# A hybrid decoder layer on one core: the attention projection cut into 32 pieces inside the recurrence, with other loads for the merge and another form of the last layer norm

## Chip, core and metric

The kernel runs on one core of a Trainium2 chip. The metric is the device time of one execution in microseconds (us), the median of several runs. All data is fp32; dense products are done as three products of a split in two parts (high and low).

## The reference, cut to what matters

One layer is computed for a prompt of 512 tokens and for 8 sequences of 4 tokens (32 sample tokens), 544 columns in all, model width 1024:

```
x = LN1(alpha*x + 1/2*gate1*SwiGLU_1(mod1(x)))
u = mod2(x);  proj = u @ w_in + b_in
y_a = rwkv7_time_mix(...)            # 8 heads x 64, recurrent state
y_b = nsa attention(...)             # 8 query heads x 64
m = (sigmoid(gA)*(y_a @ w_out_a) + sigmoid(gB)*(y_b @ w_out_b)) @ w_o
x = LN2(alpha*x + gate2*m)
x = LN3(alpha*x + 1/2*gate3*SwiGLU_2(mod3(x)))
layer_norm(x) = (x - mean) * rsqrt(var + eps) * g + b      # over the 1024 features
```

`y_a @ w_out_a` and `y_b @ w_out_b` have an inner width of 512 (four tiles of 128); SwiGLU's inner width is 2816.

## The kernel before

Activations are held feature by token: a tile has 128 features as partitions and 544 tokens as columns. A dense product of one output tile (`dense`, `dense_half`) loads a weight tile, splits it into a high part (cast on ScalarE) and a low part (subtraction on VectorE, `split`), and does three products per inner tile, on 272 columns at a time.

The program is written as generators, and the Tile framework orders each engine's instructions by a simulated list schedule: of the instructions that are ready in its model, the one first in program order goes first. On the chip each engine, and each DMA queue (SP's, ScalarE's, POOL's), then takes its instructions strictly in that order.

**Recurrence.** Four generators (`rw_head`), each for two heads of the time mixing, run interleaved, a new one starting nine steps after the last. In one of them `rw_prompt` has four solving steps (`k4`: selection products, then small VectorE operations, L1645 to L1665), steps of small 32x32 products (L1687, L1695, L1713), products of state (L1733 to L1764), a scan of seven steps (`c`: L1780, then one VectorE operation), and a tail of group norm (`rw_tail`) that ends with the split of the result into `yah`. Every step takes PSUM tiles of one bank from `smp` (`sm()`, four banks, 41 such tiles a generator) or of two banks from `mmp` (`mm()`, two buffers).

**Attention projection.** `wob_steps` (L1945 to L1980) computes, for each of 8 output tiles n, `y_b @ w_out_b` in two halves of 272 columns, each of twelve products (four inner tiles by three), evicts each with one VectorE operation (`stt`, which also applies the gate in the tile `gst`) and stores the result to DRAM (`mbd[n]`, on SP's queue). It is a generator of 16 pieces; the main loop takes a piece whenever a step of a head says `yield True`, with `high_priority(offset=300)`. Three steps of `rw_prompt` say so (after L1687, L1695 and L1713), so that 12 pieces go beside the heads and 4 (48 products) follow the loop.

**Merge.** After the recurrence `merge_load(n)` loads a tile of `w_out_a`, the gate `gdr[0, n]` and `mbd[n]`. The products (`merge_part`, L2040) of tiles 0 and 1 begin with the inner tiles 0 to 2 and end with tile 3. Each n then has two VectorE operations with the gate and `mbd`, and a split into `u`; `xT` (the residual) is loaded beside it, and the products with `w_o` follow (`last_product`, L288). The pools lie one behind the other in SBUF: the merge's `u` lies where the recurrence's `f` and sample tiles lay, its `gate` and `mb` tiles where the mask constants and the `e` tiles (the tail's) lay, `xT` where the attention's result `ybh` lay.

**Last norm.** In the last product of the second SwiGLU the columns are done in two halves of 272. `LayerNormOut` transposes each finished feature tile to tokens (L710), collects `bn_stats` (L712), and `finish` evicts each tile of tokens in two halves: ScalarE applies mean and rstd, VectorE multiplies by g (L730), POOL or VectorE adds b (L731), SP stores (L732). For the second half three tiles of tokens (two of 128, one of 32) end together after the last product.

Of the kernel before, what the change touches and what calls it, by code (L numbers as in the profile page):

```python
# [17 lines left out]
D = 1024  # L18
# [111 lines left out]
def build(tc, I, O, upto=99, dbg=None):  # L130
# [28 lines left out]
    def sm(shape=(128, 512), tag="sm"):  # L159
        return smp.tile([128, 512], F32, tag=tag, name=nm("sm"))  # L160
# [133 lines left out]
    def v272(t):  # L294
        return t.rearrange("p (a b) -> p a b", a=2)
# [313 lines left out]
    HT = TOK // 2  # L609

    def ln_prep(wk, k, h, run):

# [78 lines left out]
    class LayerNormOut:  # L691


        def __init__(self, wk, i):
            self.wk, self.t = wk, {}
            self.gb = [wk.tile([128, D], F32, name=f"lno{j}") for j in range(2)]
            for t, name in zip(self.gb, ("ln_g", "ln_b")):
                src = I[name][0, i]
                SY.dma_start(t, bass.AP(src.tensor, src.offset, [[0, 128], [1, D]]))

        def col(self, tag, n):
            return self.wk.tile([128, n], F32, tag=tag, name=nm(tag), bufs=3)

        def feature(self, qt, k):
            m = 128 if qt < 4 else NS
            if k == 0:
                self.t[qt] = ([sm(), sm()] if qt < 4 else (lambda p: [p[:, 0, :], p[:, 1, :]])(mm()),
                              self.col("lst", 12), m)
            ps, st, m = self.t[qt]
            T.transpose(ps[k // 4][:m, (k % 4) * 128:(k % 4 + 1) * 128], xT[:, k, qt * 128:qt * 128 + m], ident)  # L710
            if k % 4 == 3:
                V.bn_stats(st[:m, 6 * (k // 4):6 * (k // 4) + 6], ps[k // 4][:m])  # L712
            if k == KT - 1:
                self.finish(qt)

        def finish(self, qt):
            ps, st, m = self.t.pop(qt)
# [888 lines left out]
    def rw_prompt(ht, d):  # L1606
# [44 lines left out]
        for k4 in range(4):  # L1651
            ps = sm()
            nk = min(4, 15 - 4 * k4)
            for k in range(nk):
                T.matmul(ps[:, k * 128:(k + 1) * 128], sel[:, 4 * k4 + k, :], dd.rearrange("p q t -> p (q t)"),  # L1655
                         start=True, stop=True)
            for k_ in range(nk):
                k = 4 * k4 + k_
                n = 15 - k
                ab = ps[:, k_ * 128:(k_ + 1) * 128].rearrange("p (q t) -> p q t", t=16)  # L1660
                mul(tmp[:, :, 0:n], ab[:, :, k + 1:], bc(x16[:, :, k:k + 1], [128, 8, n]))
                sub(x16[:, :, k + 1:], x16[:, :, k + 1:], tmp[:, :, 0:n])
# [285 lines left out]
    def wob_steps():  # L1948

        for n in range(KT):  # L1950
# [41 lines left out]
    stu.close()  # L1992
    stw.close()
    yap = pool("yap")
    yah = [yap.tile([128, 4, TOK], F32R, name=f"yah{i}") for i in range(2)]
    str_ = ExitStack()
    wp, wn = pool("wps", stack=str_), 512
    rq = pool("rq", stack=str_)
# [12 lines left out]
                    next(wst, None)  # L2011
    for _ in wst:
        pass
    str_.close()
# [11 lines left out]
    u = new_u()  # L2026

    def merge_load(n):
        raw = load_raw(wview(woa, 0, 512, n * 128, (n + 1) * 128))
        t = [op.tile([128, TOK], F32, tag=tag, name=f"{tag}{n}", bufs=6) for tag in ("gate", "mb")]  # L2030
        SY.dma_start(t[0], gdr[0, n])
        SY.dma_start(t[1], mbd[n])
        return raw, t

    def merge_part(ps, w, k0, k1):
        hv, lv = w
# [4 lines left out]
                             start=(k == 0 and j == 0), stop=(k == 3 and j == 2))  # L2041


    ahead = [merge_load(n) for n in range(3)]
    parts = []
    for n in range(2):
        parts.append((mm(), split(ahead[n][0])))
        merge_part(*parts[n], 0, 3)
    for n in range(KT):
        if n + 3 < KT:  # L2050
            ahead.append(merge_load(n + 3))
        if n < 2:
            ps = parts[n][0]
            merge_part(*parts[n], 3, 4)
        else:
            ps = mm()
            merge_part(ps, split(ahead[n][0]), 0, 4)
        ga, mb = ahead[n][1]
# [49 lines left out]
    stx.close()  # L2108
    es.close()


# [47 lines left out]
```

## Time and profile before

| | us |
|---|---|
| median of 3 runs | 1773.29 |
| lowest, highest | 1766.15, 1776.47 |
| the profiled execution: its run | 1771.6 |
| the profiled execution: its span | 1769.4 |
| TensorE matmul busy in the span | 1666.9 (94%) |
| VectorE, ScalarE, POOL busy | 879.5, 603.1, 242.3 |
| mean granted TensorE clock | 0.974 |

The span runs from the first to the last instruction. Busy time of matmuls is modelled, since they are pipelined; an engine that is busy over the whole span is not one at its peak. PE is TensorE, PEld its weight loads, DVE VectorE, ACT ScalarE. A granted clock of 1.00 is 2.4 GHz, 0.50 is 1.2 GHz.

### The profile page before, as it was taken

Reading aid. Unit: us, or ns where it says so; the run is one execution under the profiler, and the core shown is the slowest. Engines: PE = TensorE matmul, PEld = TensorE weight load, DVE = VectorE, ACT = ScalarE, POOL = GpSimd, SP = SyncE. Lnnn points to the kernel's source line nnn. Section 1 sums busy time; section 2 is a strip of 40 time slices with the busy share of each in tenths; the row PEclk is TensorE's granted clock in tenths of the full one; section 3 lists DMA queues with packets and bytes.
Section 4 is the critical chain, followed back from the end, with each engine's and each line's share of the span. In section 5 each row is a group of like instructions: output and inputs, shape, how many; then the busy total and the mean of one; then the engine's idle time right before and its main releaser. Section 6 shows DMA issues by size and latency. Waiting matters only on the chain.

```text
span 1769.4 us, 34773 instructions
## 1 busy us (share of the span) xinstructions
PE 1666.9 (94%) x14710; PEld 1515.0 (86%) x14710; DVE 879.5 (50%) x1834; ACT 603.1 (34%) x1095; POOL 242.3 (14%) x290
## 2 busy tenths in 40 slices
PE   5999999999999899898998999999799999999995
PEld 4888899999999888677786978777788999999994
DVE  6664233223335736555567277675677233233345
ACT  4343221221224543334445333332456221222221
POOL 6640000000000213545300021111011000000001
PEclk9999999999999999999999989997899999999998
DMA  7863662653434285565431431201742232323321
GB/s 275 303 192 114 196 195 87 194 193 113 143 105 99 89 262 160 171 203 159 122 110 49 123 100 32 65 22 34 241 115 89 86 89 85 94 76 96 91 63 51
DMA packets 261788, 224.98 MB, mean 127 GB/s; under 512 B 28880, under 2 KB 225915, under 8 KB 261376
## 3 DMA queue, kind: packets, MB, share of 16 engines
q1 hardware_dynamic: 246008, 182.60, 34.6%
q0 software_dynamic: 9728, 33.56, 5.9%
q10 hardware_dynamic: 5896, 6.60, 1.1%
q8 instruction: 116, 1.90, 0.5%
q14 instruction: 40, 0.33, 0.1%
HBM read 199.55 MB, written 23.17 MB: 126 GB/s over the span
## 4 chain that ended last, share of the span: by engine, by line
PE 79%; DVE 7%; issue 5%; DMA 3%; ACT 3%; POOL 2%; SPq 0%; ACTq 0%; POOLq 0%; DVEq 0%
PE mm L279 45%; PE mm L288 7%; PE mm L400 5%; PE sm L519 2%; PE sm L288 2%; PE sm L1817 1%; PE mm L2040 1%; PE mm L1519 1%; POOL sraw L1217 1%; PE sm L1163 1%; PE sm L1655 1%; DMA raw<-in_phi_w1t_dram 1%; PE sm L1627 1%; PE mm L1125 1%; DVE xT L173 1%
## 5 line engine op out<-in xcount | busy, mean ns | idle before, releaser
L261 ACT CAST whi<-raw 128x1024 fp32r<-128x1024 f32 (+2 forms) x178 | 177.5, 998 | 657.9 <-PE mm L279 591.8
L279 PE MATMUL mm<-uh,whi 128*128 128x272 f32 (+1 forms) x1888 | 397.2, 292 | 2.5 <-ACT qs L193 1.3
L279 PE MATMUL mm<-uh,wlo 128*128 128x272 f32 (+1 forms) x1888 | 392.5, 289 | 0.3 <-DVE wlo L179 0.3
L279 PE MATMUL mm<-ul,whi 128*128 128x272 f32 (+1 forms) x1888 | 391.9, 288 | 0.0
L179 DVE TENSOR_TENSOR wlo<-raw,whi 128x1024 fp32r<-128x1024 f32 (+2 forms) x178 | 207.0, 1163 | 267.8 <-ACT whi L261 266.3
L279 PEld LDWEIGHTS mm<-uh,whi 128*128 128x128 f32 x1888 | 298.0, 189 | 21.8 <-ACT hh L797 9.2
L279 PEld LDWEIGHTS mm<-ul,whi 128*128 128x128 f32 x1888 | 299.8, 189 | 1.0 <-issue 1.0
L279 PEld LDWEIGHTS mm<-uh,wlo 128*128 128x128 f32 x1888 | 297.3, 189 | 1.7 <-DVE sg L173 0.8
L173 DVE TENSOR_TENSOR sg<-mm,sg 128x544 f32<-128x544 f32 (+1 forms) x47 | 32.3, 688 | 164.4 <-PE mm L279 159.4
L676 POOL TENSOR_TENSOR xT<-xT,mr 128x272 f32<-128x272 f32 x24 | 25.0, 1059 | 600.6 <-DVE xT L173 591.1
L400 PE MATMUL mm<-cx,w1h 128*128 128x256 f32 x512 | 99.8, 290 | 3.7 <-ACT cx L352 1.9
L279 PE MATMUL mm<-hh,whi 128*128 128x256 f32 x480 | 99.3, 288 | 0.0
L279 PE MATMUL mm<-hh,wlo 128*128 128x256 f32 x480 | 99.0, 288 | 0.0
L279 PE MATMUL mm<-hlo,whi 128*128 128x256 f32 x480 | 98.9, 287 | 0.0
L400 PEld LDWEIGHTS mm<-cx,w1h 128*128 128x128 f32 x512 | 82.0, 192 | 11.2 <-issue 6.7
L279 PEld LDWEIGHTS mm<-hh,whi 128*128 128x128 f32 x480 | 76.7, 188 | 1.7 <-ACT hh L797 1.7
L279 PEld LDWEIGHTS mm<-hlo,whi 128*128 128x128 f32 x480 | 76.9, 188 | 0.0
L279 PEld LDWEIGHTS mm<-hh,wlo 128*128 128x128 f32 x480 | 76.8, 188 | 0.0
L400 PE MATMUL mm<-cx,w1l 128*128 128x256 f32 x256 | 73.5, 287 | 0.0
L1217 POOL DMA_INDIRECT sraw<-in_cache_kv_sel_dram,idx x64 | 63.9, 998 | 58.1 <-DMA t_new_kv_win_sample_dram<-sraw 22.6
L182 DVE SCALAR_TENSOR_TENSOR xT<-mm,modT,xT 128x512 f32<-128x512 f32 (+2 forms) x80 | 46.3, 581 | 37.0 <-PE mm L288 37.0
L738 DVE TENSOR_TENSOR rtmp<-mm,modT 128x32 f32<-128x32 f32 x32 | 6.1, 192 | 117.0 <-PE mm L279 117.0
(529 smaller groups left out, 2959.9 us busy)
## 6 DMA issues: line engine op xcount, KB each, us to landing
araw<-in_w_ada_dram SPq DMA_DIRECT2D x56, 512.0 KB
raw<-in_ffn_w_gate_dram SPq DMA_DIRECT2D x44, 512.0 KB
raw<-in_ffn_w_up_dram SPq DMA_DIRECT2D x44, 512.0 KB
raw<-in_w_in_dram SPq DMA_DIRECT2D x36, 512.0 KB
raw<-in_ffn_w_down_dram SPq DMA_DIRECT2D x32, 448.0 KB
raw<-in_w_ada_dram SPq DMA_DIRECT2D x16, 512.0 KB
raw<-in_ffn_w_down_dram SPq DMA_DIRECT2D x16, 512.0 KB
sraw<-in_state_kv_win_dram SPq DMA_DIRECT2D x16, 256.0 KB
```

The costliest lines, as they stand in the source:

```text
L173: V.tensor_tensor(out, a, b, ALU.mult)
L179: V.tensor_tensor(out, a, b, ALU.subtract)
L182: V.scalar_tensor_tensor(out, a, s, b, o0, o1)
L261: S.copy(hv, raw)
L279: T.matmul(ps[:m, h, :n], ww[:, k, :m], xx[:, c0:c0 + n], start=(k == 0 and j == 0), stop=(k == nk - 1 and j == 2))
L288: T.matmul(ps[:, :n], ww[:, k, :], xx[:, c0:c0 + n], start=(k == 0 and j == 0), stop=(k == nk - 1 and j == 2))
L400: T.matmul(pss[:, o, 256 * v:256 * v + 256], ww[:, v, o, jj, :], xx, start=(jj == 0 and j == 0), stop=(jj == 7 and j == 2))
L519: T.matmul(hold["ps"][32 * q:32 * q + 32, :], silT[:, k, :], raws_[i][:, h * 512:(h + 1) * 512], start=(k == 0), stop=(k == KT - 1), tile_ ...
L676: G.tensor_tensor(n, n, mr, ALU.subtract)
L1125: T.matmul(ps[:, g, 0:nk], qT[64 * g:64 * g + 64, i, qt * 128:(qt + 1) * 128], kvt[br, 0][64 * g:64 * g + 64, 0:nk], start=True, stop=True)
L1163: T.matmul(acc[64 * g:64 * g + 64, kt * 128:], kvtok[br][:, kt, 128 + 64 * g:192 + 64 * g], pt_[g][:, 512 * kt:384 * kt + 512], start=(br ...
L1217: G.indirect_dma_start(out=t, out_offset=None, in_=seltab, in_offset=bass.IndirectOffsetOnAxis(ap=idx8[:, c * NB + b:c * NB + b + 1], axis=0))
```

## The change

Recurrence: `smp` is closed when the heads have been made, and opened again with three banks; the fourth bank is a pool of its own (`wbp`, one buffer) for the projection. A half of twelve products yields after six, so that there are 32 pieces; `rw_prompt` now says True at seven steps (k4 of 1 and 3, the three as before, c of 2 and 5). 28 pieces go beside the heads and 4 (24 products) follow. `mbd[n]` is stored from POOL's queue in place of SP's.

Merge: the weights of tiles 0 and 1 are loaded and split in the recurrence's own weight pool, and their products come before that pool is closed. The gate and `mbd` are loaded into `u` itself, to be overwritten by the result, four n ahead; a one-column copy on POOL makes the load of `xT[:, n]` wait for the merged tile n.

Last norm: for the second half the transposed value is x*g, left open in PSUM; sums of x and x squared over the features are done by products with ones, and one more product per half adds -mean*g + sigma*b from four rows each of g and b (high and low parts). One operation per half, on ScalarE or VectorE, then multiplies by 1/sigma. The rows of g and b are loaded and split when `LayerNormOut` is made, ahead of the second SwiGLU; they use two of the four `raw` weight buffers on the way, and six small DMAs on SP.

```diff
-    smp = pool("smp", 4, PSUM)
+    stm = ExitStack()
+    smp = pool("smp", 4, PSUM, stack=stm)
...
+            raw = wp.tile([128, wn], F32, tag="raw", name=nm("raw"), bufs=4)
+            hi = wp.tile([128, wn], F32R, tag="whi", name=nm("whi"), bufs=2)
+            rest = wp.tile([128, wn], F32, tag="raw", name=nm("raw"), bufs=4)
+            G.memset(raw, 0.0)
+            for j, name in ((0, "ln_g"), (32, "ln_g"), (64, "ln_b"), (96, "ln_b")):
+                SY.dma_start(raw[j:j + 1, :], I[name][0, i:i + 1])
+            S.copy(hi, raw)
+            sub(rest, raw, hi.bitcast(F32))
+            for a in (0, 64):
+                SY.dma_start(raw[a + 1:a + 2, :], rest[a:a + 1, :])
+            for a, sgn in ((0, -1.0), (64, 1.0)):
+                act(self.rows[a:a + 64], raw[a:a + 64], AF.Copy, scale=sgn)
...
+        def late(self, k):
+            z = xT[:, k, 256:TOK]
...
+            act(sq, z, AF.Square)
+            act(self.xs[:, k, :], z[:, 256:], AF.Copy, scale=gcol)
+            act(self.xg[k % 3], z[:, 0:256], AF.Copy, scale=gcol)
...
+                for o_, a, b in zip(self.run, self.old, (z, sq)):
+                    add(o_, a, b)
...
+            for j in range(2):
+                T.matmul(self.ps[j][k // 4][:, (k % 4) * 128:(k % 4 + 1) * 128],
+                         self.xg[k % 3][:, 128 * j:128 * j + 128], ident, is_transpose=True, start=(k % 4 == 0), stop=False)
+
+        def close(self):
...
+            for j, tag in enumerate("zq"):
...
+                T.matmul(st[:, j, 0:NL], onesr, hi, start=True, stop=False)
+                T.matmul(st[:, j, 0:NL], onesr, lo, start=False, stop=False)
+                T.matmul(st[:, j, 0:NL], onesr.bitcast(F32), self.last[j], start=False, stop=True)
+            A, B, sg, lhs = slice(0, 64), slice(64, 128), self.sg, self.lhs
+            act(sg[B], st[B, 0, 0:NL], AF.Square)
+            S.copy(lhs[A], st[A, 0, 0:NL])
+            sub(sg[B], st[B, 1, 0:NL], sg[B])
+            sub(lhs[32:64], st[32:64, 0, 0:NL], lhs[32:64].bitcast(F32))
+            act(sg[B], sg[B], AF.Sqrt, bias=eps_ln[B])
+            V.tensor_copy(lhs[B], sg[B])
+            sub(lhs[96:128], sg[96:128], lhs[96:128].bitcast(F32))
...
+            for q, dst, m, ps in out:
+                yo = self.wk.tile([128, D], F32, tag="yo", name=nm("yo"), bufs=3)
+                for hf in range(2):
+                    c = slice(512 * hf, 512 * hf + 512)
+                    T.matmul(ps[hf][:m], lhs[:, 128 * q:128 * q + m], self.rows[:, c], start=False, stop=True)
+                    if hf == 0:
+                        act(yo[:m, c], ps[hf][:m], AF.Copy, scale=r[:m, q:q + 1])
+                    else:
+                        ts(yo[:m, c], ps[hf][:m], r[:m, q:q + 1], None, ALU.mult, ALU.bypass)
+                    SY.dma_start(dst[:, c], yo[:m, c])
...
-            yield
+            yield k4 % 2 == 1
...
-            yield
+            yield c % 3 == 2
...
-                ps = sm()
-                dense_half([ps], [w], lambda k: (ybh[0][:, k, :], ybh[1][:, k, :]), 4, HT * h, HT)
+                ps = wbp.tile([128, 512], F32, tag="wb", name=nm("wb"))
+                for k in range(4):
+                    for j, (ww, xx) in enumerate(((w[0], ybh[0]), (w[0], ybh[1]), (w[1], ybh[0]))):
+                        T.matmul(ps[:, 0:HT], ww[:, k, :], xx[:, k, cs], start=(k == 0 and j == 0), stop=(k == 3 and j == 2))
+                    if k == 1:
+                        yield
...
-            SY.dma_start(mbd[n], g_)
+            G.dma_start(mbd[n], g_)
...
+    stm.close()
+    smp = pool("smr", 3, PSUM, stack=stm)
+    wbp = pool("wbp", 1, PSUM, stack=stm)
...
+    parts = [(mm(), merge_w(n)) for n in range(2)]
+    for p in parts:
+        merge_part(*p, 0, 3)
+    for p in parts:
+        merge_part(*p, 3, 4)
     str_.close()
     strp.close()
+    stm.close()
+    smp = pool("sm2", 4, PSUM, stack=stm)
...
+        if n < KT:
+            if n > 1:
+                raws[n] = load_raw(wview(woa, 0, 512, n * 128, (n + 1) * 128))
+            SY.dma_start(u[0][:, n, :].bitcast(F32), gdr[0, n])
+            SY.dma_start(u[1][:, n, :].bitcast(F32), mbd[n])
...
-        stt(v272(ga), v272(ga), 1.0, halves(ps), ALU.add, ALU.mult)
-        add(ga, ga, mb)
+        ga = op.tile([128, TOK], F32, tag="ga", name=nm("ga"), bufs=3)
+        stt(v272(ga), v272(u[0][:, n, :].bitcast(F32)), 1.0, halves(ps), ALU.add, ALU.mult)
+        add(ga, ga, u[1][:, n, :].bitcast(F32))
         S.copy(u[0][:, n, :], ga)
         sub(u[1][:, n, :], ga, u[0][:, n, :].bitcast(F32))
+
+        G.tensor_copy(xT[:, n, 0:1], ga[:, 0:1])
         SY.dma_start(xT[:, n, :], xsp[:, n, :])
...
-        for qt in ((0, 1) if h == 0 else (2, 3)):
-            lno.feature(qt, n)
+        if h:
+            lno.late(n)
+        else:
+            for qt in range(2):
+                lno.feature(qt, n)
...
-    for k in range(KT):
-        lno.feature(4, k)
+    lno.close()
```

## Rows read from the trace of the kernel before

**Rows 1.** The page's chain that ended last: shares of the span by engine.

```profile
PE 79%; DVE 7%; issue 5%; DMA 3%; ACT 3%; POOL 2%; SPq 0%; ACTq 0%; POOLq 0%; DVEq 0%
```

**Rows 2.** Stretches: busy us of PE, PEld, DVE, ACT, POOL; clock; DMA share; GB/s.

```profile
1045.00:1250.00 205.00, 196.94 (x2826) 155.73 (x2826) 138.09 (x366) 64.35 (x129) 32.46 (x40) 0.88 0.16 39
1250.00:1285.00 35.00, 27.29 (x199) 26.92 (x200) 21.07 (x35) 17.60 (x26) 0.00 (x0) 0.85 1.01 312
1345.00:1370.00 25.00, 23.16 (x179) 22.37 (x178) 19.34 (x47) 20.48 (x43) 5.65 (x6) 1.00 0.21 61
```

**Rows 3.** TensorE's waits in 1045 to 1250: us in total, times, longest.

```profile
PE sm L1687 <- DVE t L1671: 2.3, 1, 2.3
...
PE mm L1747 <- DVE f L1736: 0.2, 1, 0.2
```

**Rows 4.** Stretches of 5 us, TensorE alone: busy, granted clock, DMA share, GB/s.

```profile
1195.00:1200.00 5.00, 5.00 (x152) 1.00 0.01 3
1200.00:1205.00 5.00, 5.00 (x16) 0.51 0.01 3
1215.00:1220.00 5.00, 5.00 (x43) 0.78 0.05 9
```

**Rows 5.** Stretches of 25 us, line L288 alone (projection): busy, weight loads, clock.

```profile
1200.00:1225.00 25.00, 7.76 (x36) 7.06 (x36) 0.66 0.21 55
1225.00:1250.00 25.00, 7.54 (x48) 6.93 (x48) 0.93 0.08 19
```

**Rows 6.** Groups in 1045 to 1250: busy us, mean ns | idle before.

```profile
L182 DVE SCALAR_TENSOR_TENSOR f<-sm,wce,f 128x64 f32<-128x64 f32 x28 | 7.8, 277 | 5.2 <-PE sm L1780 5.1
L182 DVE SCALAR_TENSOR_TENSOR gst<-gst,sm 128x272 f32<-128x272 f32 x16 | 7.0, 436 | 22.6 <-PE sm L288 22.6
```

**Rows 7.** The page's group of POOL's own DMAs: busy us, mean ns | idle before.

```profile
L1217 POOL DMA_INDIRECT sraw<-in_cache_kv_sel_dram,idx x64 | 63.9, 998 | 58.1 <-DMA t_new_kv_win_sample_dram<-sraw 22.6
```

**Rows 8.** The chain that ended last, 1240 to 1284, in order of time.

```profile
1242.43 1.63 PE sm L288 x13
...
1251.26 5.61 DMA raw<-in_w_out_a_dram
...
1257.55 7.33 PE mm L2040 x42
...
1265.78 15.32 PE mm L2040 x120
```

**Rows 9.** Timeline of VectorE and TensorE around the merge: start, us, instruction.

```profile
1240.49 0.27 DVE L1804 COPY so<-sm 64x128 f32<-64x128 f32 x1
...
1250.64 0.73 DVE L179 TENSOR_TENSOR yah<-e,yah 128x544 fp32r<-128x544 f32 x1 [0.71 <-ACT yah L1927]
...
1283.93 0.29 PE L288 MATMUL mm<-uh,whi 128*128 128x272 f32 x1
```

**Rows 10.** The SP queue's waits, 1045 to 1375: us in total, times, longest.

```profile
SPq L1978 <- DVE gst L182: 76.5, 8, 32.2
```

**Rows 11.** Timeline of the end: last residual, norm, evictions, stores.

```profile
1749.24 0.19 DVE L176 TENSOR_TENSOR xT<-xT,rtmp 128x32 f32<-128x32 f32 x1
...
1752.28 2.79 ACT L193 ACTIVATE yo<-sm,lrs 128x512 f32<-128x512 f32 x4
...
1755.60 3.08 SPq L732 DMA_DIRECT2D out_y_prompt_dram<-yo  x3
...
1762.00 0.33 SPq L732 DMA_DIRECT2D out_y_sample_dram<-yo  x1
```

**Rows 12.** Timeline: single operations of the same shapes as the new norm's.

```profile
1220.50 0.73 PE L1519 MATMUL mm<-e,brk 128*128 128x272 f32 x2
...
1342.40 0.43 ACT L193 ACTIVATE sq<-xT 128x272 f32<-128x272 f32 x1 [1.64 <-DVE xT L176]
...
1344.94 0.43 DVE L179 TENSOR_TENSOR rstd<-sm,rstd 128x272 f32<-128x272 f32 x1
1345.41 0.52 ACT L193 ACTIVATE rstd<-rstd,eps_ln 128x272 f32<-128x272 f32 x1 [1.34 <-DVE rstd L179]
```

More of the change, by code (lines that the diff above doesn't have):

```diff
@@ L606, in mod_sample @@
         V.tensor_tensor(bt(out), bt(out), modT[:, sh, k, 1:9].unsqueeze(2).to_broadcast([128, NB, NT]), ALU.add)
-    HT = TOK // 2
+    HT, NL = TOK // 2, TOK - 256
     def ln_prep(wk, k, h, run):
@@ L694, in __init__ @@
         def __init__(self, wk, i):
-            self.wk, self.t = wk, {}
+            self.wk, self.t, self.i = wk, {}, i
             self.gb = [wk.tile([128, D], F32, name=f"lno{j}") for j in range(2)]
@@ L699, in __init__ @@
                 SY.dma_start(t, bass.AP(src.tensor, src.offset, [[0, 128], [1, D]]))
+            fx = [yap.tile([128, 4 * TOK], dt, tag=f"yah{j}", name=f"lnx{j}") for j, dt in enumerate((F32R, F32))]
+            self.rows, self.lhs = fx[0][:, 0:D], fx[0][:, D:D + NL]
+            o_ = 0
+            for name, n in (("xg", (256,) * 3), ("run", (NL,) * 2), ("sg", (NL,)), ("xs", (KT * NS,))):
+                setattr(self, name, [fx[1][:, o_ + sum(n[:j]):o_ + sum(n[:j + 1])] for j in range(len(n))])
+                o_ += sum(n)
+            self.sg, self.xs = self.sg[0], self.xs[0].rearrange("p (k t) -> p k t", k=KT)
+            raw = wp.tile([128, wn], F32, tag="raw", name=nm("raw"), bufs=4)
[10 more added lines that the diff above has]
+                act(self.rows[a:a + 64], raw[a:a + 64], AF.Copy, scale=sgn)
         def col(self, tag, n):
@@ new lines, in close @@
+        def close(self):
+            pair = mm()
+            for k in range(KT):
+                T.matmul(pair[:NS, k // 4, (k % 4) * 128:(k % 4 + 1) * 128], self.xs[:, k, :], ident, is_transpose=True,
+                         start=(k % 4 == 0), stop=False)
+            st = mm()
+            for j, tag in enumerate("zq"):
+                hi, lo = [lnp.tile([128, NL], F32R, tag=tag + c_, name=nm("lh")) for c_ in "hl"]
+                S.copy(hi, self.run[j])
+                sub(lo, self.run[j], hi.bitcast(F32))
+                T.matmul(st[:, j, 0:NL], onesr, hi, start=True, stop=False)
[9 more added lines that the diff above has]
+            sub(lhs[96:128], sg[96:128], lhs[96:128].bitcast(F32))
+            r = self.col("lrs", 3)
+            out = [(0, O["y_prompt"][0, 256:384, :], 128, self.ps[0]), (1, O["y_prompt"][0, 384:512, :], 128, self.ps[1]),
+                   (2, O["y_sample"].rearrange("b t d -> (b t) d"), NS, (pair[:, 0], pair[:, 1]))]
+            for q, _, m, _ in out:
+                T.transpose(st[:m, 1, 288 + 64 * q:352 + 64 * q], sg[B, 128 * q:128 * q + m], ident[B, B])
+                V.reciprocal(r[:m, q:q + 1], st[:m, 1, 288 + 64 * q:289 + 64 * q])
+            for q, dst, m, ps in out:
[8 more added lines that the diff above has]
+                    SY.dma_start(dst[:, c], yo[:m, c])
@@ L1994, in build @@
     yap = pool("yap")
-    yah = [yap.tile([128, 4, TOK], F32R, name=f"yah{i}") for i in range(2)]
+    yah = [yap.tile([128, 4, TOK], F32R, tag=f"yah{i}", name=f"yah{i}") for i in range(2)]
     str_ = ExitStack()
@@ L2013, in build, with merge_w, merge_part @@
         pass
+    def merge_w(n):
+        return load_w(wview(woa, 0, 512, n * 128, (n + 1) * 128))
+    def merge_part(ps, w, k0, k1):
+        hv, lv = w
+        for k in range(k0, k1):
+            for j, (ww, xx) in enumerate(((hv, yah[0]), (hv, yah[1]), (lv, yah[0]))):
+                for h in range(2):
+                    T.matmul(ps[:, h, 0:272], ww[:, k, :], xx[:, k, 272 * h:272 * h + 272],
+                             start=(k == 0 and j == 0), stop=(k == 3 and j == 2))
+    parts = [(mm(), merge_w(n)) for n in range(2)]
[3 more added lines that the diff above has]
+        merge_part(*p, 3, 4)
     str_.close()
     strp.close()
+    stm.close()
+    smp = pool("sm2", 4, PSUM, stack=stm)
     wp, wn = pool("wp2"), 1024
@@ L2026, in build @@
     u = new_u()
+    raws = {}
     def merge_load(n):
[L2029 to L2036, printed above, removed]
-        for k in range(k0, k1):
-            for j, (ww, xx) in enumerate(((hv, yah[0]), (hv, yah[1]), (lv, yah[0]))):
-                for h in range(2):
-                    T.matmul(ps[:, h, 0:272], ww[:, k, :], xx[:, k, 272 * h:272 * h + 272],
[L2041 to L2048, printed above, removed]
+        if n < KT:
[3 more added lines that the diff above has]
+            SY.dma_start(u[1][:, n, :].bitcast(F32), mbd[n])
+    for n in range(4):
+        merge_load(n)
     for n in range(KT):
-        if n + 3 < KT:
-            ahead.append(merge_load(n + 3))
+        merge_load(n + 4)
         if n < 2:
             ps = parts[n][0]
-            merge_part(*parts[n], 3, 4)
         else:
             ps = mm()
-            merge_part(ps, split(ahead[n][0]), 0, 4)
-        ga, mb = ahead[n][1]
-        stt(v272(ga), v272(ga), 1.0, halves(ps), ALU.add, ALU.mult)
-        add(ga, ga, mb)
+            merge_part(ps, split(raws[n]), 0, 4)
+        ga = op.tile([128, TOK], F32, tag="ga", name=nm("ga"), bufs=3)
+        stt(v272(ga), v272(u[0][:, n, :].bitcast(F32)), 1.0, halves(ps), ALU.add, ALU.mult)
+        add(ga, ga, u[1][:, n, :].bitcast(F32))
         S.copy(u[0][:, n, :], ga)
         sub(u[1][:, n, :], ga, u[0][:, n, :].bitcast(F32))
+        G.tensor_copy(xT[:, n, 0:1], ga[:, 0:1])
         SY.dma_start(xT[:, n, :], xsp[:, n, :])
@@ L2101, in final @@
     def final(h, n):
-        for qt in ((0, 1) if h == 0 else (2, 3)):
-            lno.feature(qt, n)
+        if h:
+            lno.late(n)
+        else:
+            for qt in range(2):
+                lno.feature(qt, n)
     ffn(1, u, 8, wk, [lambda k=k: ln_affine(1, k) for k in range(KT)], early, mid, down_slots, None, lnp, final)
-    for k in range(KT):
-        lno.feature(4, k)
+    lno.close()
     stx.close()
+    stm.close()
     es.close()
```

9 lines of the change are left out of this document (added).

## Prediction

> **What bounds the kernel now.** I read the chain of waits first, then the stretches, then TensorE's waits in each stretch that the change touches. The chain that ended last is TensorE for 79% of the span [rows 1], so a microsecond saved elsewhere counts only where TensorE waits for it. Three places are touched.
>
> The recurrence, 1045 to 1250, is nearly TensorE's own: it is busy for 196.94 of 205 us [rows 2], and its listed waits there are nine, from 2.3 us down to 0.2 us, 6.9 us together [rows 3]. The clock is what is left: it averages 0.88 over the 205 us [rows 2], and since it stands at 0.50 or 1.00, it was at the lower level for 24% of them, 49 us. It falls where small products run: from 1195 to 1200 TensorE executed 152 instructions at 1.00, from 1200 to 1205 it ran 16 at 0.51 [rows 4]. So a quarter of the recurrence runs at half rate, and where TensorE is the limit that costs about 25 us.
>
> The merge, 1250 to 1285, has TensorE busy for 27.29 of 35 us with the DMA engines full (share 1.01, 312 GB/s) [rows 2]. The recurrence's last `yah` is written by 1250.64 + 0.73 = 1251.4 [rows 9], but the first merge product waits for a weight load of 5.61 us issued only at 1251.26, and the first 42 take 7.33 us, 0.175 us each, against 15.32/120 = 0.128 us for the rest, because the clock had fallen in the gap [rows 8].
>
> The end, from the last residual at 1749.43 to the last store's issue at 1762.33, is 12.9 us of small work on VectorE, ScalarE and POOL with no product left [rows 11].
>
> **The recurrence, part by part.** Work is conserved: 192 products and 16 evictions of 0.436 us [rows 6] before and after. What moves is 24 products, half of the 48 behind the loop [rows 5]. At 0.125 us apiece (the merge's 0.128 us is the same shape, [rows 8]) they add 3 us to a stretch with 6.9 us of listed waits; some will fill such waits, so I take +2 us (bounds 0 and +3). Behind the loop stood 6 us of products, of which the chain shows pieces such as 1.63 us on the path [rows 8]; now 24 projection and 36 merge products stand there, 7.5 us, beside the same tail of about 13 us. I take +1 us (bounds -1 and +2).
>
> The clock may go either way and gets zero in the sum, with bounds of -12 us (half the slow time gone) and +12 us (slow time half as long again). Its rows: the 36 products of a head that went in three clusters of 12 took 7.76 us in a stretch at 0.66 [rows 5]; they were in part what brought the clock back (0.78 from 1215 to 1220, after a cluster) [rows 4]. Now 18 stand there, and 24 between the solving and scan steps, a head.
>
> The bank of its own leaves `smp` three. A k4 or scan step holds a bank until a VectorE operation such as the scan's 0.277 us has read it [rows 6]. The old projection took its banks from the same four, in the PE-bound steps; in solving and scan steps it took none, and there one bank is lost. I cost that at nothing, since no listed wait of the trace is longer than 2.3 us and all are of the heads' own data chains [rows 3]; without that cover it is the slower rival below. With one projection bank, the piece that opens a half waits for the eviction of the half before. TensorE takes its queue in order, so all head products behind it wait too. Pieces come in two head steps of one round only where one head's c of 5 meets the next head's third small step, nine steps apart: three times, at most 0.436 us plus a hand-off, so under 2 us. It is inside the bounds.
>
> The stores of `mbd` leave SP, which waited 76.5 us for their data, eight times [rows 10]. Behind those waits stood only loads for later heads and, at the end, the merge's. On POOL each costs its issue; the only DMAs of POOL in the trace are gathers of 0.998 us [rows 7], so 8 us on an engine busy for 32.46 of 205 us [rows 2]. POOL then waits for the eviction with the copies and multiplies of the next steps queued behind. I take nothing (bounds 0 and +4, half a microsecond a store).
>
> **The merge.** With SP free of `mbd`, the last recurrence DMA in its way is the state output, whose data is ready at 1240.49 + 0.27 = 1240.8 [rows 9]; the `u` tiles into which gate and `mbd` go lie over `f` tiles that the same step finishes with. So loads may start some 10 us earlier than now. Weights 0 and 1 are there before. TensorE then needs, from 1251.4, two last parts (12 products, 1.5 us) and six tiles of 24 products at 0.128 us (18.4 us): it ends at 1271.3 and the `w_o` products begin there, against 1283.93 now [rows 9]: -12.6 us. VectorE's two operations, split and low part per tile are as before. The DMA must bring 24 tiles of 272 KB, six of 256 KB and the first 512 KB of `w_o` by then: 8.8 MB, 28 us at the 312 GB/s of this stretch [rows 2]. Started at 1241 that is 1269; started at 1249.7 it is 1278, and the gain 6 us; and if the waiting `xT` loads hold back the `w_o` loads behind them on SP until the last merged tile, about nothing. Bounds -12.6 and 0; I take -11, nearest to the row of TensorE's own work, since the loads that hold SP can be ordered behind the ready ones. After that `w_o` arrives at 512 KB per 1.7 us against 3 us of products each, so what is late next is TensorE itself.
>
> **The second SwiGLU's start.** The rows of g and b cost ScalarE three operations and VectorE one, each about 1 us, and POOL a memset, in a stretch where ScalarE is busy 20.48 and VectorE 19.34 of 25 us while TensorE keeps 23.16 [rows 2]. SP waits for a split between its small DMAs, with weight loads behind. I take +0.5 us (bounds 0 and +3).
>
> **The end.** The new chain from the last residual: square 0.43; two fp32 sums of 0.73 (272 columns, as a head sum), the other four smaller ones beside them or 0.1 each; a square and a root of 0.43 and 0.52; two VectorE operations of 0.43 and two of lhs at 0.43 and 0.2; the product 0.5; three evictions of 0.70 (2.79/4, [rows 11]) on ScalarE with three on VectorE beside them; a store's issue 0.33; the single operations are in [rows 12]. That is 0.43 + 1.5 + 0.95 + 1.1 + 0.5 + 2.1 + 0.33 = 6.9 us, and eight hand-offs at an estimated 0.15 us give 8.1 against 12.9: -4.8. The stores come closer together (four of 256 KB in 2 us, at 312 GB/s 3.4 us), so the last lands up to 1 us later than its issue says. I take -4.5 (bounds -1 and -6). During the last product the extra 1 us of ScalarE and 0.9 us of VectorE a tile lie beside 3 us of products.
>
> **Sum.** +2 + 1 - 11 + 0.5 - 4.5 = -12 us on the profiled execution of 1771.6 us (span 1769.4, so 2.2 us lie around it): 1759.6. The median of the runs is 1.7 us above that execution, so 1761; I predict 1760, since the runs before lie lower as often as higher (1766.15 to 1776.47).
>
> **Rivals.** (1) The spread pieces hold the clock up. For it: the fall at 1200 comes out of a stretch of many small products [rows 4], and pieces now stand in such steps too; against: the 32x32 work itself has only six products next to it where it had twelve. Half of 49 us at full rate saves 12: 1748. (2) The merge's loads come no earlier, by SP's order or tiles still held. For it: DMA is full from 1250 on; against: the DMA share from 1195 to 1205 is 0.01 [rows 4], and SP's blocker goes. The 11 us stay: 1771. (3) Halved clusters lift the clock less. For it: the 0.78 after a cluster; against: less work remains in the slow steps. 24 us more at half rate cost 12: 1772. The page "TensorE: Matmul & The Clock Gate" of the Trainium skill, section "HAM oscillation — how this bites in real kernels", says that bursts with waits between them start slow again and again, and advises to keep products contiguous; by that rule cutting the clusters costs. The trace agrees that the clock comes back under dense products; that six are too few no run here shows. (4) Slower: three banks. Each head asks for 41 bank tiles, 164 in all; if TensorE waits for every second one by one eviction of 0.277 us [rows 6], that is 23 us: 1783. It decides from about 0.13 us a tile (21 us), where the other gains are used up and the half per cent lost. Against: no such wait is in the trace.
>
> **How the numbers follow.** Forecast 0.47, (1) 0.13, (2) 0.18, (3) 0.12, (4) 0.08, the rest 0.02. Half a per cent, 8.9 us, is what a measurement can tell from no change here: faster is below 1764.4, slower above 1782.2. Faster: 0.43 of the forecast, all of (1), 0.06 of (2) in part: 0.62. Slower: (4) and the rest, 0.10. Same: 0.28. The range takes in the middle of (1) and all of (2) and (3): 1745 to 1776.
>
> **What would show it.** Right: the first merge products of the last inner tile within 2 us of the last `yah`, at 0.128 us each; the first `w_o` product about 20 us after it; the last store's issue 8 us after the last residual; no waits of TensorE for single-bank tiles. Wrong: a SP wait in front of the `w_o` loads; a recurrence longer by over 5 us; a mean clock below 0.80 or above 0.93 in it; a gap before the third SwiGLU tile.

## The result: slower by 1.4%, with 31 us lost in the recurrence

The changed kernel takes 1795.92 us in the median of ten runs, the kernel before 1767.88 beside it: a ratio of 1.0143, with a 95% interval of 1.0117 to 1.0169. The profiled execution of the changed kernel has a span of 1793.0 us, 23.6 more than before. I forecast 1760.

By stages, read from the first and last instruction of each in the two timelines:

| Stage | before | after | difference | forecast |
|---|---|---|---|---|
| start to the last `yah` of the recurrence (start of its VectorE step) | 1250.6 | 1281.2 | +30.6 | +3 |
| from there to the last merge product | 33.2 | 26.8 | -6.4 | -11 |
| from there to the last residual (output projection, second SwiGLU) | 465.4 | 472.7 | +7.3 | +0.5 |
| last residual to the end of the span | 20.1 | 12.2 | -7.9 | -4.5 |

The chain that ended last says as little as before [rows 1]:

```profile
PE 79%; DVE 6%; issue 5%; ACT 3%; DMA 3%; POOL 3%; SPq 0%; ACTq 0%; POOLq 0%; DVEq 0%
```

The stretches that answer to [rows 2] (from:to, length, busy us and instructions of PE, PEld, DVE, ACT, POOL, granted clock, DMA share, GB/s):

```profile
1045.00:1281.00 236.00, 232.41 (x2924) 175.32 (x2924) 145.26 (x392) 69.68 (x136) 37.68 (x47) 0.84 0.14 36
1282.00:1308.00 26.00, 21.62 (x152) 21.40 (x152) 17.47 (x29) 12.00 (x19) 1.70 (x7) 0.87 0.95 297
```

The recurrence is as full as it was: TensorE is busy for 98% of it. Its waits there, against [rows 3], are even shorter (line waited at, releaser, us, times, longest):

```profile
PE sm L1864 <- DVE f L183: 0.7, 3, 0.4
PE mm L1603 <- DVE e L177: 0.6, 1, 0.6
```

All nine listed come to 3.4 us. So TensorE does not wait for 30 us more; it is busy for longer. (36 merge products stand in that window too, and none did before. They fill the tail of the last head and do not delay it: from the last products of line L1603, at 1274.80, to the last `yah` it is 6.4 us, and before, from L1519 at 1244.00, it was 6.6.) The view that shows it is the projection's own line, before and then after (from:to, length, PE busy, PEld busy, clock, DMA):

```profile
1045.00:1250.00 205.00, 34.45 (x192) 31.10 (x192) 0.88 0.16 39
```

```profile
1025.00:1281.00 256.00, 49.26 (x192) 30.63 (x192) 0.85 0.17 47
```

The same 192 products, 15 us more. The timeline of TensorE says why. Before, a piece is twelve products in a row, 0.125 us from start to start (start, duration, line, output and inputs, rows*columns of the array that the weights use, shape of the data that is moved through, count):

```profile
1164.58 0.71 PE L1890 MATMUL sm<-cst_g,s0T 128*64 128x128 f32 x5
1165.04 0.50 PE L288 MATMUL sm<-ybh,whi 128*128 128x272 f32 x2
1165.38 0.29 PE L288 MATMUL sm<-ybh,wlo 128*128 128x272 f32 x1
1165.51 0.41 PE L288 MATMUL sm<-ybh,whi 128*128 128x272 f32 x2
...
1166.63 0.49 PE L1890 MATMUL sm<-cst_g,s0T 128*64 128x128 f32 x3
```

After, single projection products stand between single 64x64 products of a head (an fp32 product leaves two records):

```profile
1145.76 0.39 PE L2059 MATMUL wb<-ybh,whi 128*128 128x272 f32 x1
1146.08 0.33 PE L1848 MATMUL mm<-f,bE 64*64 64x64 f32 x2
1146.34 0.39 PE L2059 MATMUL wb<-ybh,wlo 128*128 128x272 f32 x1
1146.66 0.33 PE L1847 MATMUL mm<-f,f 64*64 64x64 f32 x2
1146.91 0.39 PE L2059 MATMUL wb<-ybh,whi 128*128 128x272 f32 x1
```

From 1145.76 to 1146.34 is 0.58 us a round (one wide product and one small one), at full clock (the lower level begins at 1153.1). In TensorE's written order the 192 products stand in 15 runs before and in 89 after; a run is a row of them with nothing else between, and 58 of the 89 are a single product.

### The profile page after: what moved, and what is told of

The parts are those of the page before. It is cut to its first block, busy times and chain, and to the rows that moved or that the text cites. A ratio compares the mean times of both kernels' runs of the same rounds, so it can differ in the third digit from the quotient of the medians.

```text
span 1793.0 us, 34881 instructions
## 1 busy us (share of the span) xinstructions
PE 1707.9 (95%) x14727; PEld 1534.6 (86%) x14727; DVE 877.7 (49%) x1835; ACT 613.5 (34%) x1121; POOL 246.0 (14%) x304
## 4 chain that ended last, share of the span: by engine, by line
PE 79%; DVE 6%; issue 5%; ACT 3%; DMA 3%; POOL 3%; SPq 0%; ACTq 0%; POOLq 0%; DVEq 0%
PE mm L280 45%; PE mm L289 6%; PE mm L401 5%; PE wb L2059 2%; PE sm L520 2%; PE sm L1901 1%; PE mm L1603 1%; POOL sraw L1301 1%; PE sm L1711 1%; PE mm L2115 1%; PE sm L1739 1%; PE sm L1247 1%; DMA raw<-in_phi_w1t_dram 1%; DMA raw<-in_w_o_dram 1%; PE sm L1779 1%
## 5 line engine op out<-in xcount | busy, mean ns | idle before, releaser
L174 DVE TENSOR_TENSOR sg<-mm,sg 128x544 f32<-128x544 f32 (+1 forms) x47 | 32.3, 688 | 161.7 <-PE mm L280 159.2
```

The costliest lines, as they stand in the source:

```text
L174: V.tensor_tensor(out, a, b, ALU.mult)
```

## The experiments

They stand in the order of the argument, not of their numbers. Each ratio is to the kernel before, run beside it; in brackets is the 95% interval.

Theory A: the breaks cost the time. B: three small banks are too few. C: clusters of six keep the clock lower. D: the stores on POOL and the earlier weight loads of the projection stand in the heads' way.

**1. Four shared banks again.**

```
-                ps = wbp.tile([128, 512], F32, tag="wb", name=nm("wb"))
+                ps = sm()
...
-    smp = pool("smr", 3, PSUM, stack=stm)
-    wbp = pool("wbp", 1, PSUM, stack=stm)
```

> The changed kernel with one thing undone: the projection's pieces take their bank from the four shared small banks again; the 32 pieces, the seven steps, the stores on POOL, the merge and the end stay as changed. In TensorE's written order its 192 projection products now stand in 17 runs; in the changed kernel they stand in 89, 58 of them a single product between small products. Theory A (breaks): a single product takes 0.33 us to the next start against 0.125 us inside a run, and the small products beside it lose about 0.2 us more, so a break costs about 0.4 us; 72 breaks fewer give -29 us: about 1767 where the changed kernel has 1796. Theory B (three banks are too few): also about 1766. Theory C (clock: clusters of six hold it lower): the pieces are still of six, no gain, 1790 or more, unless joined pieces count as twelve. Theory D (POOL stores and earlier weight loads stand in the heads' way): 1796.

Measured: 1761.75, ratio to before 0.9971 (0.9943 to 1.0000). The last `yah` is at 1246.1. The projection's products and the whole recurrence:

```profile
1030.00:1250.00 220.00, 31.22 (x192) 27.41 (x192) 0.94 0.22 59
```

```profile
1045.00:1246.00 201.00, 195.09 (x2898) 155.31 (x2896) 141.64 (x374) 66.66 (x132) 38.57 (x48) 0.93 0.18 46
```

The whole loss is gone with the bank alone. D falls; A and B remain. C is not decided: the pieces are still of six, but two of them now mostly stand together (14 of the 17 runs are of twelve products), and that case its expectation left out. No kernel here had runs of six.

**2. The bank of its own, but pieces kept whole.**

```
+        gate.append(w1[0:1, 0, 0:1])
...
                 ps = wbp.tile([128, 512], F32, tag="wb", name=nm("wb"))
+                if gate:
+                    V.tensor_copy(ps[0:1, 0:1], gate[-1])
```

> The changed kernel with its own bank and its three small banks, 32 pieces and seven steps kept; only a VectorE copy of one element of the head's newest tile into the bank stands before the first product of a half (the product overwrites it), so that the products come late and stand together: 21 runs, 13 of them of twelve, against 89. Theory A (breaks, 0.4 us each): 68 fewer, -27 us, about 1769. Theory B (three banks): 1796. Theory C (clock by clusters of six): about 1790. Theory D (POOL stores, loads): 1796.

Measured: 1766.93, ratio 1.0002 (0.9977 to 1.0027).

```profile
1025.00:1258.00 233.00, 36.93 (x192) 31.86 (x192) 0.88 0.20 54
```

Three small banks, one projection bank, the stores on POOL and the seven steps are all as in the changed kernel, and the kernel is level with the one before. In its trace the last `yah` is at 1258.9, so 22 of the 30.6 us are gone and 8 are left. Its runs are 5 us above those of experiment 1, but they also stand 78 us at the lower clock in the median against 63, which at the 0.42 us for each that is worked out below is 6 us. So B falls as the cause of the 30 us: it was the order that the bank allowed. That the planner merges pieces that are startable in time, and keeps together those that had to wait for a shared bank, fits all orders here; its inner reason is argued, not shown.

**3. The kernel before, with its pieces broken up.**

```
-WOB_OFF = -300
+WOB_OFF = 0
```

> The kernel before with one constant changed: the projection's steps get no head start in the planner (0 for 300). Four shared banks, sixteen pieces of twelve, three steps a head, stores on SP, merge and end as before; but in TensorE's order its 192 projection products stand in 105 runs (89 of a single product) against 15. Theory A (breaks, 0.4 us each): 90 more, +36 us, about 1804. Theory B (banks): no change, 1768. Theory C (clock by size of piece): no change by the size, 1768, or less than 10 us if the breaks count as smaller clusters. Theory D: 1768.

Measured: 1834.27, ratio 1.0389 (1.0338 to 1.0439): +69 us. The direction is A's, the size nearly twice what I gave. The clock makes the rest:

```profile
1045.00:1311.00 266.00, 254.39 (x2818) 188.38 (x2818) 138.47 (x368) 64.99 (x129) 33.15 (x40) 0.74 0.12 30
```

The granted clock of 0.74 (before 0.88 [rows 2]) is 140 us at the lower level between 1000 and the last `yah`, against 51 before, 78 after and 27 in experiment 1. One profile can stray: with the very order of before, experiments 4, 9 and 10 have 51, 44 and 27. Over whole runs the medians are 183 us here, 74 for the kernel before beside it and 109 for the changed kernel.

**4. The old recurrence with the new merge and end.**

```
-            yield k4 % 2 == 1
+            yield
...
-                    if k == 1:
-                        yield
```

(and the bank as in experiment 1, and c's yield likewise)

> The changed kernel with the recurrence's bank, pieces and steps all as before (15 runs in TensorE's order, as in the kernel before); changed are then only the stores of mbd on POOL, the merge and the end. Theories A, B and C: the recurrence as before, so the gains of the merge (about -6 us by the two traces) and of the end (about -8) are left, less about 7 us lost at the start of the second SwiGLU: 1760. Theory D (POOL stores in the heads' way): the recurrence stays 20 us or more longer, 1785 or more.

Measured: 1758.47, ratio 0.9950 (0.9919 to 0.9981), as A to C said; D is out.

**8. The price of a break by itself** (a kernel that adds products behind the last residual).

```
+    for i in range(24):
+        wide()
+        small(2 * i)
+        small(2 * i + 1)
...
+    for i in range(24):
+        wide()
+        full()
```

> The kernel before with products added behind its last residual, whose result nothing reads: 120 wide products (128x128 by 272 columns, fp32r) in a row, 48 small ones (64x64, fp32) in a row, 25 wide, then 24 times two small and one wide, 24 more wide, 24 full-sized fp32 ones (128x128 by 128) and 24 times one wide and one full. Theory A: 0.125 us each in the row; beside small products a wide one takes 0.32 us and the two small ones 0.25 us against 0.03, so a round 0.57 us against 0.16 in rows. If the price is of the operand's type (fp32 beside fp32r), the full-sized fp32 ones pay it too: 0.65 us a round; if it is of the size, a round of those stays near 0.24 to 0.30 us. The whole ends about 45 us later: 1810.

Measured: 1823.24, 13 us later than I said, since the added rows themselves last 60 us (1760.1 to 1820.1). Its timeline (fp32 products leave two records each, so x4 are two small products):

```profile
1777.44 3.02 PE L2118 MATMUL sm<-pw 64*64 64x64 f32 x96
1780.39 3.40 PE L2114 MATMUL sm<-pw 128*128 128x272 f32 x25
...
1783.98 0.39 PE L2114 MATMUL sm<-pw 128*128 128x272 f32 x1
1784.30 0.33 PE L2118 MATMUL sm<-pw 64*64 64x64 f32 x4
1784.56 0.39 PE L2114 MATMUL sm<-pw 128*128 128x272 f32 x1
...
1795.69 0.59 PE L2114 MATMUL sm<-pw 128*128 128x272 f32 x1
1796.21 0.48 PE L2118 MATMUL sm<-pw 64*64 64x64 f32 x4
1796.62 0.59 PE L2114 MATMUL sm<-pw 128*128 128x272 f32 x1
...
1806.32 5.52 PE L2121 MATMUL sm<-pw 128*128 128x128 f32 x48
1811.59 0.37 PE L2114 MATMUL sm<-pw 128*128 128x272 f32 x1
1811.80 0.38 PE L2121 MATMUL sm<-pw 128*128 128x128 f32 x2
1811.94 0.37 PE L2114 MATMUL sm<-pw 128*128 128x272 f32 x1
```

In rows, 48 small ones take 1780.39 - 1777.44 = 2.95 us, 0.061 each, and a wide one 0.127: a round would be 0.25. Alternating it is 0.58: 0.33 us for going to the small shape and back. The round of the changed kernel is as long with a single small product, where the two here begin 0.01 us apart and share the time. With full-sized fp32 products a round is 0.35, and its parts in rows are 0.127 + 5.27/24 = 0.347: no price. So it is the size in use (rows*columns of the array that the weights take), not the type. And the clock gives way without any idle time (busy us and count of PE first, clock third from the right):

```profile
1785.00:1795.00 10.00, 10.00 (x89) 6.54 (x89) 0.00 (x0) 0.00 (x0) 0.00 (x0) 1.00 0.01 2
1795.00:1805.00 10.00, 10.00 (x62) 8.65 (x59) 0.00 (x0) 0.00 (x0) 0.00 (x0) 0.66 0.00 0
1805.00:1815.00 10.00, 10.00 (x89) 10.00 (x89) 0.00 (x0) 0.00 (x0) 0.00 (x0) 1.00 0.01 2
```

It fell at 1795.5, late in the alternating stretch, and a round then took 0.93; it came back at 1802.3 under the 48 wide ones in a row.

**11. Which shapes pay.**

```
+        for i in range(16):
+            wide()
+            part(k, m)          # (128, 64), (64, 128), (32, 32)
...
+    for i in range(16):
+        part(64, 64)
+        part(32, 32)
```

> The kernel before with products added behind its last residual, whose result nothing reads: wide ones (128x128 by 272, fp32r) alternating with fp32 ones of 128 columns whose weights use 128x64, 64x128 and 32x32 of the array, sixteen each in a row and sixteen alternating, with 60 wide ones between the groups; at the end sixteen of 64x64 in a row and sixteen alternating with 32x32. Theory mode (the price is for every change of the part of the array in use): each alternating round costs about 0.3 us more than its two products in rows, 64x64 beside 32x32 as well. Rival rows only (the price comes with fewer than 128 rows): 128x64 pays nothing, the other three 0.3 us. Rival wide only (only a wide product pays, for its weights can't be loaded early): 64x64 beside 32x32 pays under 0.1 us.

Measured: 1912.17 with the products added.

```profile
1778.54 3.71 PE L2121 MATMUL sm<-pw 128*64 128x128 f32 x32
...
1790.01 0.43 PE L2121 MATMUL sm<-pw 128*64 128x128 f32 x2
1790.38 0.39 PE L2114 MATMUL sm<-pw 128*128 128x272 f32 x1
1790.70 0.43 PE L2121 MATMUL sm<-pw 128*64 128x128 f32 x2
...
1858.43 0.40 PE L2121 MATMUL sm<-pw 32*32 32x128 f32 x2
1858.76 0.39 PE L2114 MATMUL sm<-pw 128*128 128x272 f32 x1
1859.08 0.40 PE L2121 MATMUL sm<-pw 32*32 32x128 f32 x2
```

A round with 128x64 takes 0.69 us where its products in rows take 0.127 + 3.63/16 = 0.354 (the 32 records of the sixteen, 1778.54 to 1782.17): +0.33. 64x128 pays 0.38 by the same reckoning, 32x32 0.30, and 64x64 beside 32x32 0.24 (0.69 against 0.455, at full clock). Theory mode holds; both rivals fall. The Trainium skill, page "TensorEngine Tiling (Array Packing)", section "Key Properties", says that changing the tiling mode, not just the tile, drains TensorE. The trace agrees in that every such change costs time, 0.24 to 0.38 us there and back; that this time is a drain, no run here shows. In this run the clock fell in three of the four alternating stretches (at 1824.2, 1861.7 and 1895.9) and came back under the wide products in a row behind the first two; with 128x64 it did not fall. In the rows of small products, each under 4 us long, it did not fall either.

Counted over TensorE's records from 1000 to the last `yah`, with sizes rounded up to 32, 64 or 128: before there are 196 changes of size, after 293, in experiment 1 192, in 2 201, in 3 356, in 4 196. The 97 changes more at 0.165 us each (half of the 0.33) are 16 us (19 at half of 0.58 - 0.127 - 0.061, the changed kernel's own round); 27 us more at the lower clock, at the 0.42 us each by which the ten runs of the changed kernel differ among themselves (span against time at the lower level, 2 x (1 - clock) x span), are 11.5 us: together 27.5 of the 30.6. By the same two prices experiment 3 has 26 and 37 us, 63 together, where its last `yah` (1311.5) comes 61 us later than before. Experiments 1, 2 and 4 come out 5 to 6 us later than these prices give (last `yah` at 1246.1, 1258.9 and 1255.8), so the reckoning, an estimate, is good to about that.

**5 to 7, 9 and 10: the rest of the change.** Where the 7.3 us behind the merge go was read from the start of every 48th wide product in the traces: +2.3 at the first `w_o` products, +1.8 at the third SwiGLU tile, +0.9 spread over the long middle, +2.1 in the last down products, beside the late norm's new conversions. In experiment 5 the kernel of experiment 1 has the rows of g and b split in the tiles of `yah` (the expectation says the attention output, but the edit takes those of `yah`):

```
-            raw = wp.tile([128, wn], F32, tag="raw", name=nm("raw"), bufs=4)
...
+            raw, rest, hi = fx[1][:, 0:D], fx[1][:, D:2 * D], self.rows
```

> The first experiment's kernel (the change with the projection in the four shared banks) and one thing more: the last norm's rows of g and b are split in the tiles that held the attention output, not in buffers of the weight ring, so neither the POOL memset nor SP's two small row copies stand behind weight buffers. In the first experiment's trace the 600th wide product behind the merge starts 93.8 us after it, in the kernel before 87.8, of which 2.7 us come at the third SwiGLU tile. Theory rows (SP stands at the row copies for 22.8 us with the next weight load behind it): the 2.7 us go, so 1759 where the first experiment had 1762. Rival (the conversions of ScalarE and VectorE themselves hold that tile up): no change, 1762.

Measured: 1762.23, ratio 0.9949 (0.9923 to 0.9975). The step at that tile is gone (+2.1 ahead of it and behind it), so SP's stand at the row copies was the cause. The time itself can't tell this from experiment 1 (0.9949 and 0.9971, with intervals that overlap). These are SP's waits in the changed kernel between 1300 and 1400; the second has the tile's weight load behind it:

```profile
SPq L716 <- POOL raw L714: 30.3, 1, 30.3
SPq L720 <- DVE sg L174: 22.8, 1, 22.8
```

In experiment 6, built on experiment 5, POOL issues the reloads of `xT` as well:

```
-        SY.dma_start(xT[:, n, :], xsp[:, n, :])
+        G.dma_start(xT[:, n, :], xsp[:, n, :])
```

> As the kernel with the rows apart, and the eight reloads of xT are issued by POOL behind its own marker copies, not by SP. Theory queue: SP waits for each marker (13.4 us in seven waits in the changed kernel) with w_o loads behind them, and the 200th wide product behind the merge starts 33.7 us after it against 30.4 before; with the reloads on POOL these 3.3 us go: 1756. Rival (the DMA engines are full there, share 0.95 to 1.00, so w_o cannot land sooner): no change against the kernel with the rows apart, 1759.

Measured: 1771.40, ratio 0.9992 (0.9964 to 1.0019). A miss, and worse than the rival: the merge takes 32.3 us against 27.1 in experiment 5. Its runs also stand 81 us at the lower level in the median, against 67. TensorE's longest wait behind the recurrence, in experiment 5 and then here:

```profile
PE mm L2110 <- ACT whi L262: 4.4, 1, 4.4
```

```profile
PE mm L2110 <- ACT whi L262: 6.9, 2, 4.4
```

The merge's weights come later. That the reloads, no longer held back on SP, take their share of full DMA engines (1.11 from 1265 to 1275, against 0.85) is the likely reason; it was not taken apart further.

Experiment 7 has both repairs and the whole pieces in a bank of their own.

> The changed kernel with its own bank, 32 pieces and seven steps, and three repairs: the one-element copy that keeps the pieces whole, the rows apart, the reloads on POOL. If the own bank costs nothing once the pieces are whole (theory A), it equals the four-bank kernel of the same call but for the clock: 1761, 6 us under the second experiment's 1767. If three banks or the DVE copy cost something, 1766 or more.

Measured: 1776.92, ratio 1.0025 (0.9990 to 1.0060). That misses its own mark, 1761. Its merge takes 29.6 us, against 24.8 in experiment 2, so the loss of experiment 6 is in it, and its runs stood 92 us at the lower clock in the median against 81. Whether the bank of its own costs a few us even with whole pieces, through the clock, stays open.

Experiments 9 and 10 join the old recurrence, the new merge and end and the rows apart, with `mbd` stored from POOL (9) and from SP (10):

```
-            G.dma_start(mbd[n], g_)
+            SY.dma_start(mbd[n], g_)      # experiment 10 alone
```

> The recurrence as in the kernel before (four banks, sixteen pieces of twelve, three steps a head, 15 runs of projection products) but for the stores of mbd on POOL; merge and end as changed; the last norm's rows apart. By stages of the traces: merge 7 us shorter, start of the second SwiGLU 5 us longer (the fourth experiment had 8, the rows apart gave 2.5 back), end 7.5 us shorter: -9.5 us and a ratio of 0.9945. If the POOL stores cost the recurrence 4 us (my upper bound of them), 0.997.

> As the kernel above, but mbd is stored from SP again. If POOL stores cost nothing and free SP (my step), this one is up to 6 us slower, by the merge's loads that come later behind SP's waits for mbd: 1.000. If stores on POOL hold up POOL's copies in the recurrence, it is faster, 0.993 or less. If both are hidden, the same within 0.2%.

Measured: 1766.16, ratio 0.9963 (0.9937 to 0.9988), and 1764.15, ratio 0.9961 (0.9934 to 0.9987). The queue of the stores makes no difference, and the merge stage is as short with either (25.6 and 25.5 us). Both beat the kernel before by 0.4%, and the changed one by 1.8% (1.0143 / 0.9963); the lowest ratio, 0.9949, is experiment 5's, not to be told apart from these.

## Why the prediction was wrong

**The step that failed** is the first one: "Work is conserved: 192 products", "at 0.125 us apiece", +2 us with bounds of 0 and +3. The count held; the price did not. 0.125 us is a product's price behind one of its own kind, taken from the merge's row of 120 [rows 8]. I moved the products into steps full of 64x64 and 32x32 work and let them keep it. What the runs showed in its place: 0.58 us for a round of one such product and two small ones, against 0.25 in rows (experiment 8), and a recurrence longer by 30.6 us where I had +3. The trace of before could hardly warn: it has fifteen runs. I took the pieces' wholeness for a property of the code; experiment 1 against the changed kernel shows that it hung on the bank.

**The clock**: zero with bounds of ±12 us. Its share of the loss, 11.5 us, is at the upper bound, and the third rival (24 us more at half rate) had the size: 27. But that is in part luck: its reason, clusters of six for twelve, was never run, for the pieces did not stand as sixes but mostly as single products, and in experiment 1 they joined to twelves. The Trainium skill's page "TensorE: Matmul & The Clock Gate", section "HAM oscillation — how this bites in real kernels", advises to keep products contiguous, and that points the right way; experiment 3 agrees with 0.74. Here the clock fell with TensorE busy throughout, not in waits.

**Three banks and one projection bank**: at nothing and under 2 us. Right by the waits, since all nine together are 3.4 us, and experiment 2 ends level with the kernel before. The fourth rival had the sign, but not the mechanism.

**Stores on POOL**: nothing, right, by experiments 9 and 10, though POOL stood long at them (waits from 1030 to 1285; before, [rows 10], it was SP):

```profile
POOL mbd L2066 <- DVE gst L183: 88.9, 6, 27.7
```

**The merge**: -11, measured -6.4, within the bounds. The products of the last inner tile do start within 2 us of `yah`. What was over-rated is the loads: I had them start 10 us ahead of the last `yah`; SP issued the third weight at 1281.20, with the last `yah`, and from then on the DMA engines were full (0.95 and 297 GB/s above). The trace has what held them. SP was done with the state output at 1272.9 and issued one load; the next, of `mbd`, stood until 1279.30:

```profile
SPq L2145 <- DMA mbd<-gst: 5.8, 1, 5.8
```

POOL issued the last store of `mbd` at 1276.88, and it landed at 1279.28; why the first load of `mbd` waits for the last store, no run here shows. So SP's freedom from the stores, on which the step stood, gave nothing: experiment 10 stores from SP and merges as fast. What [rows 8] showed of before is here (start, length, what):

```profile
1287.66 16.77 PE mm L2115 x113
1305.99 6.41 DMA raw<-in_w_o_dram
1314.76 6.98 DMA raw<-in_w_o_dram
1322.93 16.42 PE mm L289 x126
```

The first `w_o` product comes 26 us behind `yah`, not 20, and 2.3 us are given back at the loads, as the second rival said in part.

**The second SwiGLU**: +0.5, measured +1.8 at its start, within the bounds; but +0.9 and +2.1 further on were not in the sum: I had laid the last norm's conversions beside the down products for nothing.

**The end**: -4.5, measured -7.9. The direction held, and so did the single prices (lines that answer to [rows 11]):

```profile
1780.73 0.51 ACT L194 ACTIVATE lnx<-xT,pv 128x256 f32<-128x256 f32 x1 [2.06 <-DVE rtmp L833]
1784.92 0.26 PE L787 MATMUL mm<-cst_g,lnx 64*128 64x64 f32 x1 [1.97 <-ACT lnx L194]
1786.48 0.69 ACT L194 ACTIVATE yo<-sm,lrs 128x512 f32<-128x512 f32 x1 [1.62 <-PE sm L793]
1789.26 1.16 SPq L798 DMA_DIRECT2D out_y_sample_dram<-yo  x2
```

The last two issues begin 8.3 us behind the last residual (1780.77 + 0.19 to 1789.26) and end at 1790.4, 9.5 behind it, where I gave 8.1. Of this, 0.4 us is an error of my sum: four operations of 0.43, 0.43, 0.43 and 0.2 us stand in it as 1.1, and they come to 1.5. So the norm itself gave 3.4 us (12.9 to 9.5), not 4.8, and that the whole stage gave 7.9 is luck. The other 4.5 us lie behind the last issue: from its end to the span's end it was 1769.4 - 1762.33 = 7.1 us before and is 2.6 now, where I had let it grow by up to 1. It is not the landing of the stores: the last packets of data end 1.0 us behind the last issue in both traces. Before, what ended last was POOL, which adds b there. The `DRAIN` behind its last addition, the longest of these, stood for 9612 ns from 1759.0, to 1768.6, while SP's waits for the stores were over at 1763.9 (durations in ns min/median/max, first and last start):

```profile
L2155 POOLq DRAIN  x3: 40/102/9612, 1759.0 to 1769.2; - x3
```

In the changed kernel POOL has no work in the last step. Its `DRAIN` is as long, but it begins 30 us before the last issue:

```profile
L2258 POOLq DRAIN  x3: 40/102/10273, 1760.2 to 1792.7; - x3
```

Experiment 3, with the old norm, has the 7.1 us too, and experiments 1, 2 and 4, with the new one, have 2.5 to 2.6. No run moved POOL's additions alone.

## What to carry to other kernels

Price a moved product by its neighbours in the new place, not by a row of its own kind: where it stands alone between products of another array size, add about a third of a microsecond and ask what the clock does. Before giving filler work a buffer of its own, look at the written order of the engine: a shared buffer that made it wait may be what kept it together. With TensorE busy throughout and no waits in the view, compare busy time for the same number of instructions. At the end of a kernel, look at which engine is the last to finish, not only at the last store.

## What the runs showed of the hardware

A change of the array size in use costs 0.24 to 0.38 us there and back at full clock, with none for a change of type at full size (experiments 8 and 11). The clock can fall in a stretch where TensorE is never idle (1.00 to 0.66 above), and it came back under wide products in a row. POOL's last `DRAIN` lasts 9.6 to 10.3 us from the start of POOL's last operation, which itself takes 1.65 us (the two rows above); in the kernel before the end of the program waited for it. The time at the lower level also makes most of the scatter of one kernel: over 25 runs of the kernel before, the spans go from 1758.5 to 1775.4 us while that time goes from 60 to 103, 0.38 us of span for each (0.43 and 0.46 in the two other sets of 25 and 23 runs).
